# Column means of an 8192 x 8192 matrix: loads in pairs of row groups, the last four groups summed on TensorE alone

## The chip, the core and the metric

The kernel runs on one core of a Trainium2 chip. The time is device time in microseconds. The engines named below are TensorE (PE, its weight loads PEld), VectorE (DVE), ScalarE (ACT), GpSimd (POOL) and SyncE (SP), which here issues the loads and most of the stores. Data move between the chip's main memory and the on-chip memory through 16 DMA engines.

## The reference

```python
def setup_inputs():
    return {"x": np.random.randn(8192, 8192).astype(np.float32)}

def reference(x):
    return np.mean(x, axis=0)
```

The input has 268.4 MB and is read once. The output has 32 KB.

## The kernel before

The 8192 rows are 64 groups of 128 rows (one row of a group per partition, 4 MB a group). A block is 512 columns (`F`), so a group has 16 blocks; `W` is a quarter of a block. `bufs` (L51) holds six rows of 8192 floats per partition: four are landing places, `both` (L52) takes the sum of two of them, `acc` (L53) is the running sum.

Loads all go through `load` (L75) on SP's queue. A load names as its wait the add that reads its buffer last, and each even load from the ninth on also the two loads eight and seven places before it. SP works in order, so a load that waits holds all that are written behind it.

- L111 to L113: the first loads are the last two blocks of group 60 into the tile `early` (512 KB), groups 0 to 3 in one load of 16 MB, groups 4 and 5 in one of 8 MB, and blocks 9 to 13 of group 63 into `early` (1280 KB).
- L114 to L116: VectorE adds groups 0 and 1 to 2 and 3 in an add of 16,384 columns, then 4 and 5 onto these in another (the result lies in `both` and `acc`), and `both` onto `acc`.
- L120 to L133: groups 6 to 55 come in pairs, 8 MB a load, two neighbouring rows of the matrix (64 KB in one stretch) per partition. For each pair VectorE adds the two rows into `both` and `both` into `acc`. After the pairs 24 and 32, GpSimd adds the early pieces of group 63 into `acc` (L129).
- L135 to L138: groups 56 to 59 come one by one; one add each.
- L139 to L144: group 60 is loaded without its last two blocks and added in blocks 0 to 13; of group 61 blocks 7 to 15 are added.
- L146 to L152: group 62 is loaded whole; GpSimd adds its blocks 14, 15 and 8 into `acc` (L148). Group 63 then comes in pieces: blocks 4 to 7, 0 to 3, 14 and 15, and 8.

The function `add` (L94) lets a no-op of ScalarE or GpSimd (L99) wait for the load and for the add ahead, and the add waits for that no-op alone.

TensorE sums over the 128 partitions: a matmul with a 128 x 32 matrix of 1/8192 (`ones`) puts the column sums of up to 512 columns into one of four strips of 32 partitions (L183; each matmul appears as two instructions). Which block goes when is the list `sums`, written by `blocks` (one block per strip) and `spread` (several blocks cut into four equal parts). Its order (L167 to L181) begins with blocks 2 to 4 and 0 to 1 of `acc` and blocks 0 to 6 of group 61, and ends with the pieces of group 63. Four tiles of accumulators fill up: `banks` (blocks 0 to 3, 4 to 7), `wide` (blocks 9 to 13), `two` (14, 15) and `last` (8).

ScalarE copies the accumulators out (L209 to L213; the copies lie inside `both`), VectorE the last one (L214), and five stores write the result, two from ScalarE's queue and three from SP's (L210, L216 to L219). At the end SP waits for loads and stores (`landed`, L220 to L224), and VectorE for one store (L225).

Of the kernel before, what the change touches and what calls it, by code (L numbers as in the profile page):

```python
# [9 lines left out]
def kernel(  # L10
# [2 lines left out]
    x: bass.AP,  # L13
    out: bass.AP,
):

    nc = tc.nc
    f32 = mybir.dt.float32
    M, N = x.shape  # L40
    P = nc.NUM_PARTITIONS
    F = 512
    W = F // 4
    G = M // P
    U = 6
    sync = mybir.DependencyInfo(mybir.DependencyClass.Sync, mybir.DependencyReason.DATA)

    sb = ctx.enter_context(tc.tile_pool(name="sb", bufs=1))
    psp = ctx.enter_context(tc.tile_pool(name="psum", bufs=1, space=bass.MemoryType.PSUM))

    bufs = sb.tile([P, U, N], f32, name="bufs")  # L51
    both = bufs[:, U - 2, :]  # L52
    acc = bufs[:, U - 1, :]  # L53
    ones = sb.tile([P, 32], f32, name="ones")
    early = sb.tile([P, 7 * F], f32, name="early")
    tail = sb.tile([P, W], f32, name="tail")
    warm = sb.tile([P, 32], f32, name="warm")
    nc.gpsimd.memset(ones[:], 1.0 / M)  # L58
    ready = sb.tile([P, 1], f32, name="ready")
    tc.keep_in_program_order(  # L60
        nc.gpsimd.tensor_add(out=ready[:], in0=ones[:, 0:1], in1=ones[:, 1:2]))  # L61
    banks = [psp.tile([P, F], f32, name=f"bank{b}") for b in range(2)]
    wide = psp.tile([P, 2 * F], f32, name="wide")
    two = psp.tile([P, 2 * W], f32, name="two")
    last = psp.tile([P, W], f32, name="last")

    loads = []

    def landed(*inss):

        nop = tc.keep_in_program_order(nc.sync.nop()).ins
        for o in inss:
            tc.add_manual_dep(nop, o.name, sync, reason="SyncE waits")

    def load(dst, src):  # L75
        ins = tc.keep_in_program_order(nc.sync.dma_start(out=dst, in_=src)).ins  # L76
        k = len(loads)
        over = loads[k - 8:k - 6] if k >= 8 and k % 2 == 0 else []
        tc.declare_no_dep(ins, group="loads", keep=over, reason="the reader of the buffer waited")
        for o in over:  # L80
            tc.add_manual_dep(ins, o.name, sync, reason="covers the next load too")
        tc.add_to_no_dep_group("loads", ins)
        loads.append(ins)
        return ins

    def rows(g, n=1):
        return x[g * P:(g + n) * P, :]

    def load_rows(g, u, n):
        return load(bufs[:, u:u + n, :], rows(g, n).rearrange("(p j) c -> p j c", j=n))  # L90

    adds, joins = [], {}

    def add(dst, a, b, dmas):  # L94

        ins = nc.vector.tensor_add(out=dst, in0=a, in1=b).ins  # L96
        if dmas and adds:
            waiter = nc.scalar if len(adds) % 8 > 1 else nc.gpsimd
            nop = joins[waiter] = tc.keep_in_program_order(waiter.nop()).ins  # L99
            for o in dmas + adds[-1:]:  # L100
                tc.add_manual_dep(nop, o.name, sync, reason="the no-op waits")
            for group in ("loads", "adds"):
                tc.declare_no_dep(ins, group=group, reason="the no-op waited")
            tc.add_manual_dep(ins, nop.name, sync, reason="waits for both at once")
        elif adds:
            tc.declare_no_dep(ins, group="loads", reason="the add ahead waited")
        tc.declare_no_dep(ins, group="early", reason="the no-op waited, or the add behind it")
        tc.add_to_no_dep_group("adds", ins)
        adds.append(ins)

    load(early[:, 5 * F:], rows(G - 4)[:, 14 * F:])  # L111
    first, second = load_rows(0, 0, 4), load_rows(4, 4, 2)
    load(early[:, :5 * F], rows(G - 1)[:, 9 * F:14 * F])  # L113
    add(bufs[:, 2:4, :], bufs[:, 2:4, :], bufs[:, 0:2, :], [first])  # L114
    add(bufs[:, 4:6, :], bufs[:, 4:6, :], bufs[:, 2:4, :], [second])
    add(acc, acc, both, [])  # L116
    tc.keep_in_program_order(nc.scalar.copy(out=warm[:], in_=ones[:]))  # L117
    ahead = []
    g = 6
    while g < G - 8:  # L120
        u = (g + 2) % 4
        dma = load_rows(g, u, 2)
        add(both, bufs[:, u, :], bufs[:, u + 1, :], [dma])
        add(acc, acc, both, ahead)
        ahead = []
        if g in (24, 32):
            lo, hi = (0, 4) if g == 24 else (4, 7)
            cols = slice((9 + lo) * F, (9 + hi) * F)
            ins = tc.keep_in_program_order(nc.gpsimd.tensor_add(  # L129
                out=acc[:, cols], in0=acc[:, cols], in1=early[:, lo * F:hi * F])).ins  # L130
            tc.add_to_no_dep_group("early", ins)
            ahead = [ins]
        g += 2  # L133

    while g < G - 4:  # L135
        row = bufs[:, (g + 2) % 4, :]
        add(acc, acc, row, [load(row, rows(g))])
        g += 1  # L138
    for lo, hi, loaded in [(0, 14, 14), (7, 16, 16)]:  # L139
        row = bufs[:, (g + 2) % 4, :]  # L140
        dma = load(row[:, :loaded * F], rows(g)[:, :loaded * F])
        cols = slice(lo * F, hi * F)
        add(acc[:, cols], acc[:, cols], row[:, cols], [dma])
        g += 1  # L144
    r61, r62, r63 = [bufs[:, (g + 1 + j) % 4, :] for j in range(3)]
    load(r62, rows(g))  # L146
    for cols in [slice(14 * F, 16 * F), slice(8 * F, 9 * F)]:
        joined = tc.keep_in_program_order(nc.gpsimd.tensor_add(  # L148
            out=acc[:, cols], in0=acc[:, cols], in1=r62[:, cols])).ins
    g += 1  # L150
    for lo, hi in [(4, 8), (0, 4), (14, 16), (8, 9)]:
        load(r63[:, lo * F:hi * F], rows(g)[:, lo * F:hi * F])  # L152

    sums = []

    def blocks(row, lo, hi):
        for i in range(lo, hi):
            sums.append((banks[i // 4], i % 4, 0, row[:, i * F:(i + 1) * F]))

    def spread(dst, row, lo, hi, part=slice(None)):  # L160
        n = (hi - lo) * W
        for c in range(0, n, F)[part]:
            for q in range(4):
                at = lo * F + q * n + c
                sums.append((dst, q, c, row[:, at:at + min(F, n - c)]))

    blocks(acc, 2, 5)  # L167
    blocks(acc, 0, 2)
    blocks(r61, 0, 7)
    blocks(acc, 5, 8)  # L170
    blocks(r62, 0, 8)
    spread(wide, acc, 9, 14, slice(1))
    blocks(r63, 4, 8)
    spread(wide, r62, 9, 14, slice(1))
    for row in (acc, r62):
        spread(wide, row, 9, 14, slice(1, 2))
    spread(two, acc, 14, 16)
    blocks(r63, 0, 4)
    spread(last, acc, 8, 9)
    spread(two, r63, 14, 16)  # L180
    spread(last, r63, 8, 9)  # L181
    for n, (dst, q, c, cols) in enumerate(sums):
        summed = tc.keep_in_program_order(nc.tensor.matmul(  # L183
            out=dst[32 * q:32 * q + 32, c:c + cols.shape[1]],
# [5 lines left out]
            skip_group_check=True,  # L190
        )).ins

    res = both[:, :2 * F].rearrange("p (b c) -> p b c", b=2)
    res5 = both[:, 2 * F:2 * F + 5 * W]
    res2 = both[:, 4 * F:4 * F + 2 * W]

    def copy(dst, src):
        return tc.keep_in_program_order(nc.scalar.copy(out=dst, in_=src)).ins  # L198

    def store(engine, dst, src, *then):  # L200
        ins = tc.keep_in_program_order(engine.dma_start(out=dst, in_=src)).ins
        for o in then:
            tc.add_manual_dep(ins, o.name, sync, reason="follows that load")
        return ins

    def part(lo, hi):
        return out[lo * F:hi * F].rearrange("(q c) -> q c", q=4)

    copy(res[:, 1, :], banks[1][:])  # L209
    s1 = store(nc.scalar, part(4, 8), res[0:P:32, 1, :], loads[-4])  # L210
    copy(res5, wide[:, :5 * W])
    copy(res[:, 0, :], banks[0][:])
    copied = copy(res2, two[:])  # L213
    ended = nc.vector.tensor_copy(out=tail[:], in_=last[:]).ins  # L214
    landed(*joins.values())
    s5 = store(nc.sync, part(9, 14), res5[0:P:32, :], *loads[-7:-3])  # L216
    s0 = store(nc.sync, part(0, 4), res[0:P:32, 0, :])
    s2 = store(nc.scalar, part(14, 16), res2[0:P:32, :])
    store(nc.sync, part(8, 9), tail[0:P:32, :])  # L219
    landed(loads[-2], joined)  # L220
    landed(loads[-1], copied)
    landed(s0, s5)
    landed(s1, summed)
    landed(s2, ended)  # L224
    hold = tc.keep_in_program_order(nc.vector.nop()).ins  # L225
    tc.add_manual_dep(hold, s0.name, sync, reason="VectorE ends late")

# [29 lines left out]
```

## Time and profile before

| | us |
|---|---|
| median of 3 runs | 628.55 (627.99 to 628.99) |
| profiled execution, first to last instruction (span) | 626.4 |
| median run less the span | 2.15 |
| VectorE busy, 60 instructions | 529.3 |
| TensorE busy, 126 matmul instructions | 13.3 |
| GpSimd busy | 12.0 |
| ScalarE busy | 3.7 |
| read from main memory | 268.44 MB, 429 GB/s over the span |

The profiled execution has no time of its own beside its span; what lies around the span is taken from the median of the runs. In the profile, times count from the start of the span. A line of the chain has a start, a duration, and the engine, tile and line that ran then, or "DMA" for the time from a load's issue to its landing. A line of the timeline has a start, a duration, engine, line, operation, tiles, the number of instructions merged, and in brackets how long the engine had been idle and what ended that. L96 is VectorE's add, L76 a load, L99 the no-op, L183 a matmul, L201 a store.

### The profile page before, as it was taken

How to read it: one execution, taken by the hardware profiler on the slowest of the kernel's cores; microseconds unless marked ns; L12 is line 12 of the kernel's file. 1: busy time of each engine (PE TensorE's matmuls, PEld its weight loads, DVE VectorE, ACT ScalarE, POOL GpSimd, SP SyncE). 2: the span in 40 equal slices, each digit the busy share in tenths (PEclk: the TensorE clock that was granted, in tenths of full speed). 3: DMA queues.
4: the chain of work that ended last, by engine and by line, in shares of the span. 5: the costliest groups of instructions: out<-in, count | busy, mean ns of one | idle time of the engine just before them, and what ended most of it. 6: DMA issues, size and time to landing. Idle time of an engine off the chain costs nothing.

```text
span 626.4 us, 484 instructions
## 1 busy us (share of the span) xinstructions
PE 13.3 (2%) x126; PEld 4.0 (1%) x126; DVE 529.3 (85%) x60; ACT 3.7 (1%) x6; POOL 12.0 (2%) x10
## 2 busy tenths in 40 slices
PE   0000000000000000000000000000000000000008
PEld 0000000000000000000000000000000000000002
DVE  0028999998888998889998899888898888999992
ACT  0000000000000000000000000000000000000001
POOL 0000000000000000020000200000000000000002
PEclk9999999999999999999999999999999999999999
DMA  8999999999999999999999999999999999999997
GB/s 372 465 402 428 459 410 460 402 469 402 469 402 469 402 469 402 469 402 469 402 465 406 439 431 427 444 410 460 402 469 402 469 402 469 402 435 435 419 435 305
DMA packets 5930, 268.50 MB, mean 429 GB/s; under 512 B 660, under 2 KB 668, under 8 KB 1064
## 3 DMA queue, kind: packets, MB, share of 16 engines
q1 hardware_dynamic: 5912, 268.46, 99.3%
q8 instruction: 1, 0.02, 0.0%
q10 hardware_dynamic: 16, 0.01, 0.0%
q14 instruction: 1, 0.01, 0.0%
HBM read 268.44 MB, written 0.03 MB: 429 GB/s over the span
## 4 chain that ended last, share of the span: by engine, by line
DMA 59%; DVE 30%; another core or an unknown queue 10%; issue 0%; SPq 0%; ACTq 0%; PE 0%; POOL 0%; POOLq 0%
DMA bufs<-in_x_dram 59%; DVE bufs L96 30%; SPq L76 0%; ACTq L99 0%; PE last L183 0%; DVE tail L214 0%; POOL ready L61 0%; POOL ones L58 0%; POOLq L99 0%; POOLq L241 0%
## 5 line engine op out<-in xcount | busy, mean ns | idle before, releaser
L96 DVE TENSOR_TENSOR bufs<-bufs 128x8192 f32<-128x8192 f32 (+3 forms) x59 | 529.0, 8966 | 85.9 <-DMA bufs<-in_x_dram 43.0
L183 PE MATMUL bank<-bufs,ones 128*32 128x512 f32 x62 | 10.0, 716 | 610.3 <-DVE bufs L96 610.0
L129 POOL TENSOR_TENSOR bufs<-bufs,early 128x2048 f32<-128x2048 f32 (+1 forms) x2 | 7.9, 3954 | 348.5 <-DVE bufs L96 348.5
L148 POOL TENSOR_TENSOR bufs<-bufs 128x1024 f32<-128x1024 f32 (+1 forms) x2 | 3.6, 1824 | 258.9 <-DMA bufs<-in_x_dram 258.9
L214 DVE COPY tail<-last 128x128 f32<-128x128 f32 x1 | 0.3, 291 | 8.8 <-PE last L183 8.8
L183 PEld LDWEIGHTS bank<-bufs,ones 128*32 128x32 f32 x62 | 2.2, 121 | 616.4 <-issue 614.5
L198 ACT COPY bufs<-bank 128x512 f32<-128x512 f32 x2 | 1.2, 586 | 617.9 <-PE bank L183 617.9
L183 PE MATMUL wide<-bufs,ones 128*32 128x512 f32 (+1 forms) x32 | 2.5, 432 | 0.0
L117 ACT ACT_TABLE_LOAD x1 | 1.3, 1283 | 0.7 <-PEq L241 0.7
L183 PE MATMUL two<-bufs,ones 128*32 128x256 f32 x16 | 1.2, 380 | 0.0
L183 PEld LDWEIGHTS wide<-bufs,ones 128*32 128x32 f32 x32 | 1.0, 110 | 1.8 <-issue 1.8
L183 PE MATMUL last<-bufs,ones 128*32 128x128 f32 x16 | 0.8, 279 | 0.1
L198 ACT COPY bufs<-wide 128x640 f32<-128x640 f32 x1 | 0.7, 692 | 1.1 <-PE wide L183 1.1
L183 PEld LDWEIGHTS last<-bufs,ones 128*32 128x32 f32 x16 | 0.4, 109 | 1.2 <-issue 0.6
L183 PEld LDWEIGHTS two<-bufs,ones 128*32 128x32 f32 x16 | 0.4, 109 | 0.1
L198 ACT COPY bufs<-two 128x256 f32<-128x256 f32 x1 | 0.4, 372 | 0.1
L117 ACT COPY warm<-ones 128x32 f32<-128x32 f32 x1 | 0.2, 217 | 0.0
L61 POOL TENSOR_TENSOR ready<-ones 128x1 f32<-128x1 f32 x1 | 0.2, 193 | 0.1
L58 POOL MEMSET ones<- 128x32 f32 x1 | 0.1, 125 | 0.3 <-POOLq L241 0.3
L241 POOL MEMSET const-float32-0.0<- 128x1 f32 x1 | 0.1, 98 | 0.2 <-issue 0.2
L241 POOL MEMSET const-bfloat16-1.0<- 128x1 bf16 x1 | 0.1, 102 | 0.0
L241 POOL MEMSET const-uint8-127<- 128x1 uint8 x1 | 0.1, 102 | 0.0
(1 smaller groups left out, 0.1 us busy)
## 6 DMA issues: line engine op xcount, KB each, us to landing
bufs<-in_x_dram SPq DMA_DIRECT2D x6, 4096.0 KB, 20.4
bufs<-in_x_dram SPq DMA_DIRECT2D x1, 3584.0 KB
bufs<-in_x_dram SPq DMA_DIRECT2D x2, 1024.0 KB, 18.7
early<-in_x_dram SPq DMA_DIRECT2D x1, 1280.0 KB
early<-in_x_dram SPq DMA_DIRECT2D x1, 512.0 KB
bufs<-in_x_dram SPq DMA_DIRECT2D x1, 512.0 KB, 19.4
bufs<-in_x_dram SPq DMA_DIRECT2D x27, 29.9
bufs<-in_x_dram SPq DMA_DIRECT2D x1, 256.0 KB, 19.7
```

The source lines that it names most:

```text
L58: nc.gpsimd.memset(ones[:], 1.0 / M)
L61: nc.gpsimd.tensor_add(out=ready[:], in0=ones[:, 0:1], in1=ones[:, 1:2]))
L96: ins = nc.vector.tensor_add(out=dst, in0=a, in1=b).ins
L117: tc.keep_in_program_order(nc.scalar.copy(out=warm[:], in_=ones[:]))
L129: ins = tc.keep_in_program_order(nc.gpsimd.tensor_add(out=acc[:, cols], in0=acc[:, cols], in1=early[:, lo * F:hi * F])).ins
L148: joined = tc.keep_in_program_order(nc.gpsimd.tensor_add(out=acc[:, cols], in0=acc[:, cols], in1=r62[:, cols])).ins
L183: summed = tc.keep_in_program_order(nc.tensor.matmul(out=dst[32 * q:32 * q + 32, c:c + cols.shape[1]], lhsT=ones[:], rhs=cols, start=all(( ...
L198: return tc.keep_in_program_order(nc.scalar.copy(out=dst, in_=src)).ins
L214: ended = nc.vector.tensor_copy(out=tail[:], in_=last[:]).ins
L241: nc = _bacc.Bacc("TRN2", target_bir_lowering=False, num_devices=1)
```

## The change

There are no early loads and no tile `early`. All groups up to 61 are loaded in pairs, the first pair too; the places of the pairs alternate (buffers 0 and 1, 2 and 3). Each of the pairs up to 58 is added by VectorE as before in the middle of the kernel, the first straight into `acc`; so VectorE sums groups 0 to 59. Pair 60 is loaded and not added. Group 62 is loaded whole, group 63 in pieces of blocks 0 to 7, 8 to 12, 13 and 14, and 15. GpSimd adds nothing.

TensorE takes all 16 blocks of group 60, of 61, of `acc`, of 62 and of 63, in this order. The accumulators hold blocks 0 to 3, 4 to 7, 8 to 12, 13 and 14, and 15. The copies go to tiles of their own; VectorE copies the second accumulator and the last, ScalarE the other three, all after the whole list of matmuls is written. Four stores go by SP, that of blocks 13 and 14 by ScalarE, and the stores no longer name loads to follow.

```diff
-    load(early[:, 5 * F:], rows(G - 4)[:, 14 * F:])
-    first, second = load_rows(0, 0, 4), load_rows(4, 4, 2)
-    load(early[:, :5 * F], rows(G - 1)[:, 9 * F:14 * F])
-    add(bufs[:, 2:4, :], bufs[:, 2:4, :], bufs[:, 0:2, :], [first])
-    add(bufs[:, 4:6, :], bufs[:, 4:6, :], bufs[:, 2:4, :], [second])
-    add(acc, acc, both, [])
+    def pair(g):
+        u = g % 4
+        dma = load(bufs[:, u:u + 2, :], rows(g, 2).rearrange("(p j) c -> p j c", j=2))
+        return bufs[:, u, :], bufs[:, u + 1, :], dma
+
+    a, b, dma = pair(0)
+    add(acc, a, b, [dma])
...
+    for g in range(2, G - 4, 2):
+        a, b, dma = pair(g)
+        add(both, a, b, [dma])
+        add(acc, acc, both, [])
+    r60, r61, _ = pair(G - 4)
+    r62, r63 = bufs[:, 2, :], bufs[:, 3, :]
+    load(r62, rows(G - 2))
+    for lo, hi in [(0, 8), (8, 13), (13, 15), (15, 16)]:
+        load(r63[:, lo * F:hi * F], rows(G - 1)[:, lo * F:hi * F])
...
+    def spread(dst, row, lo, n):
+        for c in range(0, n * W, F):
             for q in range(4):
-                at = lo * F + q * n + c
-                sums.append((dst, q, c, row[:, at:at + min(F, n - c)]))
+                at = lo * F + q * n * W + c
+                sums.append((dst, q, c, row[:, at:at + min(F, n * W - c)]))
...
+    for row in (r60, r61, acc, r62, r63):
+        blocks(banks[0], row, 0)
+        blocks(banks[1], row, 4)
+        spread(banks[2], row, 8, 5)
+        spread(banks[3], row, 13, 2)
+        spread(last, row, 15, 1)
...
+    copy(0)
+    nc.vector.tensor_copy(out=res[1][:], in_=banks[1][:])
+    copy(2)
+    copied = copy(3)
     ended = nc.vector.tensor_copy(out=tail[:], in_=last[:]).ins
     landed(*joins.values())
...
+    s0 = store(nc.sync, 0, 4, res[0])
+    s4 = store(nc.sync, 4, 8, res[1])
+    s8 = store(nc.sync, 8, 13, res[2])
+    s13 = store(nc.scalar, 13, 15, res[3])
+    store(nc.sync, 15, 16, tail)
+    landed(loads[-2])
     landed(loads[-1], copied)
-    landed(s0, s5)
-    landed(s1, summed)
-    landed(s2, ended)
+    landed(s0, s4)
+    landed(s8, summed)
+    landed(s13, ended)
```

More of the change, by code (lines that the diff above doesn't have):

```diff
@@ L54 @@
     ones = sb.tile([P, 32], f32, name="ones")
-    early = sb.tile([P, 7 * F], f32, name="early")
     tail = sb.tile([P, W], f32, name="tail")
+    res = [sb.tile([P, w], f32, name=f"res{i}") for i, w in enumerate((F, F, 5 * W, 2 * W))]
     warm = sb.tile([P, 32], f32, name="warm")
@@ L61 @@
         nc.gpsimd.tensor_add(out=ready[:], in0=ones[:, 0:1], in1=ones[:, 1:2]))
-    banks = [psp.tile([P, F], f32, name=f"bank{b}") for b in range(2)]
-    wide = psp.tile([P, 2 * F], f32, name="wide")
-    two = psp.tile([P, 2 * W], f32, name="two")
+    banks = [psp.tile([P, w], f32, name=f"bank{b}") for b, w in enumerate((F, F, 2 * F, 2 * W))]
     last = psp.tile([P, W], f32, name="last")
@@ L87, in rows @@
         return x[g * P:(g + n) * P, :]
-    def load_rows(g, u, n):
-        return load(bufs[:, u:u + n, :], rows(g, n).rearrange("(p j) c -> p j c", j=n))
     adds, joins = [], {}
@@ L106, in add @@
             tc.declare_no_dep(ins, group="loads", reason="the add ahead waited")
-        tc.declare_no_dep(ins, group="early", reason="the no-op waited, or the add behind it")
         tc.add_to_no_dep_group("adds", ins)
         adds.append(ins)
-    load(early[:, 5 * F:], rows(G - 4)[:, 14 * F:])
-    first, second = load_rows(0, 0, 4), load_rows(4, 4, 2)
-    load(early[:, :5 * F], rows(G - 1)[:, 9 * F:14 * F])
-    add(bufs[:, 2:4, :], bufs[:, 2:4, :], bufs[:, 0:2, :], [first])
-    add(bufs[:, 4:6, :], bufs[:, 4:6, :], bufs[:, 2:4, :], [second])
@@ L116 @@
-    add(acc, acc, both, [])
-    tc.keep_in_program_order(nc.scalar.copy(out=warm[:], in_=ones[:]))
[L118 to L149, printed above, removed]
@@ L150 @@
-    g += 1
-    for lo, hi in [(4, 8), (0, 4), (14, 16), (8, 9)]:
-        load(r63[:, lo * F:hi * F], rows(g)[:, lo * F:hi * F])
-    sums = []
[L156 to L162, printed above, removed]
-            for q in range(4):
-                at = lo * F + q * n + c
-                sums.append((dst, q, c, row[:, at:at + min(F, n - c)]))
@@ L167 @@
[L167 to L181, printed above, removed]
+    def pair(g):
+        u = g % 4
+        dma = load(bufs[:, u:u + 2, :], rows(g, 2).rearrange("(p j) c -> p j c", j=2))
+        return bufs[:, u, :], bufs[:, u + 1, :], dma
@@ new lines, with blocks @@
+    a, b, dma = pair(0)
+    add(acc, a, b, [dma])
+    tc.keep_in_program_order(nc.scalar.copy(out=warm[:], in_=ones[:]))
+    for g in range(2, G - 4, 2):
[7 more added lines that the diff above has]
+        load(r63[:, lo * F:hi * F], rows(G - 1)[:, lo * F:hi * F])
+    sums = []
+    def blocks(dst, row, lo):
+        for q in range(4):
+            sums.append((dst, q, 0, row[:, (lo + q) * F:(lo + q + 1) * F]))
@@ L191, with copy, store @@
         )).ins
[L193 to L213, printed above, removed]
+    def copy(i):
+        return tc.keep_in_program_order(nc.scalar.copy(out=res[i][:], in_=banks[i][:, :res[i].shape[1]])).ins
+    def store(engine, lo, hi, src):
+        dst = out[lo * F:hi * F].rearrange("(q c) -> q c", q=4)
+        return tc.keep_in_program_order(engine.dma_start(out=dst, in_=src[0:P:32, :])).ins
+    copy(0)
+    nc.vector.tensor_copy(out=res[1][:], in_=banks[1][:])
+    copy(2)
+    copied = copy(3)
     ended = nc.vector.tensor_copy(out=tail[:], in_=last[:]).ins
     landed(*joins.values())
[L216 to L220, printed above, removed]
+    s0 = store(nc.sync, 0, 4, res[0])
[4 more added lines that the diff above has]
+    landed(loads[-2])
     landed(loads[-1], copied)
-    landed(s0, s5)
-    landed(s1, summed)
-    landed(s2, ended)
+    landed(s0, s4)
+    landed(s8, summed)
+    landed(s13, ended)
     hold = tc.keep_in_program_order(nc.vector.nop()).ins
```

## The prediction

> **What bounds the kernel now.** I read the page's busy line, its DMA queues and its chain first, then the chain in order of time, then the timeline of the last 14 us, then the groups by shape. The page:
>
> ```profile
> PE 13.3 (2%) x126; PEld 4.0 (1%) x126; DVE 529.3 (85%) x60; ACT 3.7 (1%) x6; POOL 12.0 (2%) x10
> q1 hardware_dynamic: 5912, 268.46, 99.3%
> ```
>
> The load queue q1 moves packets for 99.3% of 626.4 us, that is 622.0 us; the other 4.4 us are the start before the first packet and the stores' end. No load ever waits long enough for the queue to run dry. VectorE is at 85% and has no share in the rate. The chain in order of time:
>
> ```profile
> 472.10 8.70 DVE bufs L96
> 480.80 0.02 issue
> 480.82 29.93 DMA bufs<-in_x_dram
> 510.75 0.03 ACTq L99
> 510.79 0.02 issue
> 510.81 8.70 DVE bufs L96
> 519.51 0.02 issue
> 519.53 29.92 DMA bufs<-in_x_dram
> 549.44 0.04 ACTq L99
> ...
> 603.45 19.74 DMA bufs<-in_x_dram
> 623.19 0.04 issue
> 623.23 0.47 PE last L183 x8
> 623.70 0.02 issue
> 623.73 0.29 DVE tail L214
> ```
>
> Each 8 MB load is issued when the add that frees its two rows ends, and lands 29.9 us later, because the load ahead of it is still moving. Landings 510.75 and 549.44 are four groups apart: 38.69 us, or 9.673 us per group. The pieces of "DVE" in this chain are therefore no bound: they end 10.6 us before the queue would be empty (29.93 less the 19.35 that a pair moves). What ends the run is the last piece's landing at 623.19, then eight matmuls, one copy, one store. The timeline of TensorE near the end:
>
> ```profile
> 616.28 1.92 PE L183 MATMUL bank<-bufs,ones 128*32 128x512 f32 x16 [0.28 <-DMA bufs<-in_x_dram]
> 618.02 1.04 PE L183 MATMUL wide<-bufs,ones 128*32 128x512 f32 x8
> 618.88 1.04 PE L183 MATMUL bank<-bufs,ones 128*32 128x512 f32 x8
> 619.74 1.48 PE L183 MATMUL wide<-bufs,ones 128*32 128x512 f32 x24
> 621.03 0.61 PE L183 MATMUL two<-bufs,ones 128*32 128x256 f32 x8
> 621.46 1.04 PE L183 MATMUL bank<-bufs,ones 128*32 128x512 f32 x8
> 623.73 0.29 DVE L214 COPY tail<-last 128x128 f32<-128x128 f32 x1 [8.83 <-PE last L183]
> 624.04 0.50 SPq L201 DMA_DIRECT2D out_dram<-tail  x1
> ```
>
> Starts give TensorE's pace: eight instructions of 512 columns 0.86 us (618.02 to 618.88), eight of 256 columns 0.43 (621.03 to 621.46), sixteen of 128 columns 0.43 (1.29 less 0.86). The sums start at 609.98, and there the weight loads show four instructions per 0.86 us (half pace) until 613.41, four per 0.43 after it. 616.28 is also the landing of group 62.
>
> **The change part by part.** All sums are made against the profiled execution, span 626.4; the median run is 628.55, so 2.15 us lie outside the span, and I keep them.
>
> *The load stream.* The bytes stay the same, so only packet sizes and gaps count. The trace's packet records give the time of one packet: 64 KB 2.420 us, 32 KB 1.218, 10 KB 0.385 median and 0.420 mean (all 128 in the early piece), 8 KB 0.313, 4 KB 0.159 median and 0.193 mean, 2 KB 0.084; each load has eight per DMA engine. The check: group 63's eleven blocks in pieces of 4, 4, 2 and 1 give 8 x (0.313 + 0.313 + 0.159 + 0.084) = 6.95, and the landings 616.28 and 623.23 are 6.95 apart.
> - Early pieces removed: 8 x 0.193 + 8 x 0.420 = 4.90 us leave the stream ahead of group 56. In before, 549.44 is the landing of groups 0 to 55 and the early pieces, so after it is 544.54. The slow mean of the 4 KB piece may belong to being first and not to its size; then 8 x (0.193 - 0.159) = 0.27 stays with the first pair. With a rest for the unlike start I take 0 to 0.33 us back.
> - Groups 56 to 61 become three pairs: 6 x 9.673 = 58.04, landing of pair 60 at 602.58. Single groups cost (616.28 - 549.44) / 6.875 = 9.722 each, so pairs save 0.05 apiece.
> - Group 62 stays single: 9.72, at 612.30.
> - Group 63 now brings all 16 blocks as 8, 5, 2, 1. A 16 KB packet isn't in the loads; a line through 10 KB and 28 KB (0.385 and 1.067) gives 0.613. 8 x (0.613 + 0.385 + 0.159 + 0.084) = 9.93, or 10.21 with the early piece's 0.420. Last landing 622.23.
> - With both upper ends, 622.84. Before it was 623.23. So the stream ends 0.39 to 1.00 us earlier; I take 0.70, the middle, since neither excess has a second row.
>
> *Queues.* There are 36 loads for 40; the load of a pair waits for the add that reads its rows, as before. At the start only pairs 0 and 2 are queued (39 us of work); pair 0 lands near 21.9, VectorE adds it in 8.7, and the third pair is issued near 31, some 10 us before the queue ends. At the end group 62 and all pieces of 63 wait for the first add of pair 58 (landing 583.2, add 8.7: 591.9), while pair 60 is still moving until 602.6. That is the cover; without it each microsecond of lateness would be one of time. The five issues take about 0.35 us each and hold nobody.
>
> *VectorE.* 59 adds of 8192 columns at 8.70, two per pair, 17.4 of each 19.35. POOL's two adds of early pieces (4.49 and 3.42) leave, and with them the longer adds beside them; both were under the stream. acc is complete at 583.2 + 17.5 = 600.7, and TensorE wants it at 611.4. POOL's two adds of group 62 leave as well.
>
> *TensorE.* 240 matmul instructions for 126. One row is 3 x 0.86 (eight blocks and the wide part of five) + 0.22 + 0.43 + 0.22 = 3.44 us. It starts at pair 60's landing, cold: 16 instructions at half pace cost 1.72 more. Rows 60, 61, acc, 62 and the first eight blocks of 63 take 1.72 + 4 x 3.44 + 1.72 = 17.2 us. The stream brings blocks 8 to 12 of group 63 at 9.72 + 4.90 + 3.08 = 17.7 us after pair 60. So TensorE arrives 0.5 us ahead and the last landing rules again: then 0.47 for the last eight, as before. To the end TensorE needs 17.2 + 1.08 + 0.43 + 0.47 = 19.2 us, the stream 19.65 + 0.47 = 20.1. The cover is 0.9 us; this is the thin place of the change.
>
> The trace shows one warm-up, 3.43 us at half pace (609.98 to 613.41), while the page's clock row says 1.00 throughout. [...]
>
> *Copies and stores.* ScalarE copies bank 0 (0.59) early, VectorE bank 1: no row, between the 0.29 of 128 columns and the 0.69 of ScalarE's 640; I take 0.69. Both are over before 621.5. The copy of the wide bank (0.69) ends near 622.3, its store on SP (0.63, from "622.43, two in 1.26") near 622.9; the tail's store wants SP at 623.34. So it isn't held up, with 0.4 us to spare; if it is, 0.1 to 0.5 us are paid. The VectorE hold now waits for a store that is long over: 0, at most 0.1 either way.
>
> Sum: last landing -0.70, the rest as before: tail's store issued at 623.34 for 624.04, span 625.7, with 2.15 outside it 627.85. I write 627.9.
>
> **The rivals.**
> [...]
> - *TensorE far behind (slower).* It decides from 2.9 us of extra TensorE work, that is 0.9 of cover and 2.0 from 627.85 to 629.81: a half pace of 9.2 us or more, or eight wide instructions in 1.0 us instead of 0.86. [...] Half pace to the end would give 34.4 for 20.1: 642. For it: rows of four groups in one uninterrupted run, which this trace never shows while five loads move. Against it: at 616.28 to 622.3 the pace held while loads moved.
> - *The stream is slower at the pairs' rate.* 0.03 us more per group over 62 groups would add 1.9 to 627.85: 629.8. For it: single slices of the page swing from 402 to 469 GB/s. Against it: 38.69 and 38.70 repeat from 123.7 to 549.4, two and two pairs.
> - *The early pieces cost more than their packets* (a turn of the queue at start or at 62 us): another 0.6 off, 627.2, faster. For it: the first 10 us move 367 GB/s. Against it: the start has no reason to end with them.
> - *No effect at all*, the upper ends taken and the tail's store held up: 628.3, inside the forecast's own width.
>
> **How the numbers follow.** About 0.2%, 1.26 us, is what a measurement can tell from no change here: faster is under 627.29, slower over 629.81. Chances: forecast 0.57 (its own range 627.2 to 628.7), one window more 0.14, TensorE far behind 0.13, slower stream 0.08, early pieces dearer 0.08. Faster: the last and 0.04 of the forecast's low side, 0.12. Slower: 0.13 and 0.08, and 0.01 of the one-window case, 0.22. Same: 0.66. The range reaches from 627.1 (1.00 off and 0.45 for runs that differ by 0.5 from their median) to 630.2, which takes in the slower stream and part of TensorE far behind, and leaves out less than 2 in 10.
>
> **What would show it.** Right: landing of pair 60 at 602.6 to 603.0, group 62 at 612.3 to 612.8, the last piece at 622.2 to 622.9; q1 again over 99%; TensorE's first matmul right at pair 60's landing, with waits on DMA in group 63; VectorE's last add near 600.7. [...]

## The result, and the profile after

The changed kernel takes 629.64 us (median of 16 runs, 629.14 to 630.35), the kernel before 628.50 in the same runs: ratio 1.002, interval 1.0013 to 1.0026. It is slower by 1.1 us, where 0.7 us of gain was forecast. The median span went from 626.4 to 627.65; what lies outside the span stayed at 1.9 to 2.0. So the loss is inside the span. The page of the changed kernel (span 627.8):

```profile
PE 20.5 (3%) x240; PEld 8.0 (1%) x240; DVE 513.8 (82%) x61; ACT 3.1 (0%) x5; POOL 0.5 (0%) x6
q1 hardware_dynamic: 5216, 268.47, 99.1%
q8 instruction: 2, 0.03, 0.0%
q14 instruction: 1, 0.01, 0.0%
```

The loads are again over 99% of the span. The two lines below them are instruction fetches: packets of 16 KB on q8 and of 8 KB on q14, which by the order of the packets (sorted into 16 rows further down) go through the same 16 DMA engines as the loads. Before had one of each on its page too, and their place in time is what counts. The trace's packet records put before's at 622.6 us (q8, around the last landing) and 626.0 (q14, after all stores), and after's at 462.5 (q14), 615.6 and 623.5 (q8). The chain of the changed kernel, in order of time:

```profile
457.45 30.69 DMA bufs<-in_x_dram
488.14 0.03 ACTq L70
...
496.92 29.92 DMA bufs<-in_x_dram
...
535.62 29.94 DMA bufs<-in_x_dram
...
574.33 29.92 DMA bufs<-in_x_dram
604.25 0.14 issue
604.39 6.09 PE bank L118 x40
610.47 0.22 PE last L118 x8
610.69 3.22 PE bank L118 x40
```

One load, that issued at 457.45, took 30.69 us for the 29.92 of the loads behind it: 0.77 late, with the 8 KB packet at 462.5 in it, and nothing behind it won the time back. Pair 60 landed at 604.25; 602.58 to 602.9 was forecast. Group 63's pieces, behind the 16 KB packet at 615.6, in the timeline (start, duration, line, operation, and in brackets what the engine waited for):

```profile
622.57 0.16 PEld L118 LDWEIGHTS bank<-bufs,ones 128*32 128x32 f32 x8 [0.74 <-DMA bufs<-in_x_dram]
623.81 0.16 PEld L118 LDWEIGHTS bank<-bufs,ones 128*32 128x32 f32 x8 [0.22 <-DMA bufs<-in_x_dram]
624.44 0.16 PEld L118 LDWEIGHTS last<-bufs,ones 128*32 128x32 f32 x8 [0.48 <-DMA bufs<-in_x_dram]
625.25 0.51 SPq L133 DMA_DIRECT2D out_dram<-tail  x1
```

TensorE waits for all three last pieces, so the loads still set the end. The last one came at 624.44, before's at 623.23: 1.21 of the profiled 1.4 us. The other 0.2 us lie behind the issue of the tail's store, which is at 625.25 for 624.04 and so 1.21 late too. TensorE was not far from setting the end itself: it began the sums of group 63 at 620.83 and had 3.22 us of work before the last eight, so it could have started these at 624.05 at the earliest.

### The profile page after: what moved, and what is told of

It reads as the page before. It is cut to its first block, busy times and chain, and to the rows that moved or that the text cites. A ratio compares the mean times of both kernels' runs of the same rounds, so it can differ in the third digit from the quotient of the medians.

```text
span 627.8 us, 690 instructions
## 1 busy us (share of the span) xinstructions
PE 20.5 (3%) x240; PEld 8.0 (1%) x240; DVE 513.8 (82%) x61; ACT 3.1 (0%) x5; POOL 0.5 (0%) x6
## 3 DMA queue, kind: packets, MB, share of 16 engines
q1 hardware_dynamic: 5216, 268.47, 99.1%
## 4 chain that ended last, share of the span: by engine, by line
DMA 75%; DVE 21%; PE 3%; issue 0%; ACTq 0%
DMA bufs<-in_x_dram 75%; DVE bufs L67 21%; PE bank L118 3%; PE last L118 0%; ACTq L70 0%; DVE tail L139 0%
## 5 line engine op out<-in xcount | busy, mean ns | idle before, releaser
L67 DVE TENSOR_TENSOR bufs<-bufs 128x8192 f32<-128x8192 f32 x59 | 512.8, 8692 | 89.5 <-ACTq L70 41.8
L118 PE MATMUL bank<-bufs,ones 128*32 128x512 f32 (+2 forms) x200 | 20.0, 546 | 604.4 <-DMA bufs<-in_x_dram 604.4
L118 PEld LDWEIGHTS bank<-bufs,ones 128*32 128x32 f32 x200 | 6.9, 120 | 615.5 <-issue 614.5
L129 ACT COPY res<-bank 128x512 f32<-128x512 f32 (+2 forms) x3 | 1.6, 550 | 621.1 <-PE bank L118 621.1
L118 PE MATMUL last<-bufs,ones 128*32 128x128 f32 x40 | 2.1, 275 | 0.0
## 6 DMA issues: line engine op xcount, KB each, us to landing
bufs<-in_x_dram SPq DMA_DIRECT2D x31, 29.9
```

Of the source, the lines that this page charges most:

```text
L118: summed = tc.keep_in_program_order(nc.tensor.matmul(out=dst[32 * q:32 * q + 32, c:c + cols.shape[1]], lhsT=ones[:], rhs=cols, start=all(( ...
L129: return tc.keep_in_program_order(nc.scalar.copy(out=res[i][:], in_=banks[i][:, :res[i].shape[1]])).ins
```

## The experiments

Four theories were put against each other. A: TensorE's 16 KB fetch holds one DMA engine's share of the loads, and a load lands with its slowest engine. B: the loads in pairs, at the start above all, are slower by themselves. C: TensorE's longer list is the loss. D, after the first four runs: the 8 KB fetch belongs to VectorE's program and costs in the same way. The table has what the runs gave; "last" is where the last eight matmuls start in the profiled execution, 0.04 or 0.05 us behind the last piece's landing in every kernel but e2; the fetches are from the packet records (us from the start of the span, those before 630).

| kernel | time, us (before beside it) | median span | TensorE (weight loads with it), VectorE instructions | 8 KB at | 16 KB at | last |
|---|---|---|---|---|---|---|
| before | 628.5 | 626.4 | 252, 60 | 626.0, 628.1 | 622.6 | 623.23 |
| after | 629.64 (628.50) | 627.65 | 480, 61 | 462.5 | 615.6, 623.5 | 624.44 |
| e1_before_extra_fetch | 629.60 (628.33) | 627.7 | 508, 60 | 627.6, 629.6 | 343.4, 622.6 | 624.64 |
| e2_after_head_of_before | 632.01 (628.33) | 630.2 | 480, 59 | 628.7 | 617.8, 625.2 | 626.52 |
| e3_after_two_rows_summed | 629.72 (628.33) | 627.0 | 192, 61 | 462.4 | 629.0 | 623.81 |
| e4_before_head_in_pairs | 628.94 (628.33) | 627.1 | 252, 62 | 466.5, 628.4 | 622.2 | 623.87 |
| f1_after_copy_on_scalar | 630.60 (628.39) | 628.7 | 480, 60 | 626.2 | 614.3, 623.6 | 624.42 |
| f2_before_one_more_vector | 629.18 (628.39) | 627.2 | 252, 61 | 485.7, 628.9 | 622.2 | 623.74 |
| f3_after_no_fetch | 629.98 (628.39) | 627.5 | 192, 60 | 624.8 | 629.4 | 623.02 |
| g1_after_scalar_copy_hold | 629.39 (628.34) | 627.4 | 480, 60 | 627.3 | 614.6, 623.4 | 624.05 |
| g2_after_loads_63_sums | 630.25 (628.34) | two groups | 252, 60 | 626.0 | 622.2 | 622.84 |
| g3_before_no_hold | 629.39 (628.34) | 627.4 | 252, 60 | 625.6, 629.4 | 622.6 | 623.30 |
| h1_after_loads_60_sums | 630.16 (628.29) | two groups | 240, 60 | 626.0 | 622.0 | 622.92 |
| h2_after_loads_63_again | 628.60 (628.29), one execution | 626.7 | 252, 60 | 626.4 | 622.4 | 623.27 |
| h3_after_loads_early_pe | 630.44 (628.10) | 628.5 | 252, 60 | 626.1 | 622.0 | 624.27 |
| h4_after_loads_no_fetch_hold | 629.15 (628.31) | 626.3 | 192, 60 | 626.0 | 628.6 | 622.95 |

**One fetch more on the kernel before.** 64 small products after the add of pair 30:

```diff
+        if g == 30:
+            for i in range(64):
+                extra = tc.keep_in_program_order(nc.tensor.matmul(
+                    out=spare[0:32, 0:32], lhsT=ones[:], rhs=ones[:], start=True, stop=True, ...))
+                if i == 0:
+                    tc.add_manual_dep(extra, adds[-1].name, sync, ...)
```

> The kernel before, with 64 small matmuls (256 TensorE instructions, a 32 x 32 product each, result unused) that run after the add of pair 30. Theory A (instruction fetches share the DMA engines with the loads: one 16 KB fetch packet, 1.07 us in the changed kernel's trace, holds one engine's load queue for about 0.5 us, and a load lands with its slowest engine): one fetch packet of 16 KB appears near 310 us, the next landings come 0.4 to 1.0 us late and stay late, time 0.4 to 1.0 us over the kernel before. Theory B (the loss is in the start and the first loads): within 0.2 us of the kernel before. Theory C (TensorE's tail is the loss): within 0.2 us.

It came 1.27 us over the kernel before (ratio 1.0020, 1.0011 to 1.0028). The chain, in order of time, has the price at one place:

```profile
289.90 27.43 DMA bufs<-in_x_dram
326.11 31.34 DMA bufs<-in_x_dram
366.23 29.93 DMA bufs<-in_x_dram
```

The load with the 16 KB packet at 343.4 lands 1.4 us late (31.34 for 29.93), and the loads behind it keep the delay. A holds, dearer than its range by a little, with the packet at 343.4 and not near 310; B and C, which gave nothing here, don't explain this run.

**The head of before on the changed kernel.** Groups 0 to 5 in loads of 16 and 8 MB:

```diff
+    first, second = load_rows(0, 0, 4), load_rows(4, 4, 2)
+    add(bufs[:, 2:4, :], bufs[:, 2:4, :], bufs[:, 0:2, :], [first])
+    add(bufs[:, 4:6, :], bufs[:, 4:6, :], bufs[:, 2:4, :], [second])
+    add(acc, acc, both, [])
...
-    for g in range(2, G - 4, 2):
+    for g in range(6, G - 4, 2):
```

> The changed kernel with the first six groups loaded as before, 16 MB and 8 MB, and added in two wide adds; no early pieces, tail as changed. Theory A (instruction fetches): at most 0.4 us faster than the changed kernel, so 0.7 to 1.2 us over the kernel before. Theory B (start and first loads, which moved 0.8 us between the forecast landing of ten groups, 99.58, and the measured 100.38): 0.6 to 0.9 us faster than the changed kernel, 0.2 to 0.5 us over the kernel before. Theory C (TensorE's tail): no change, 1.1 over.

All three theories missed: the median is 3.7 us over the kernel before, and the profiled execution, the slowest of the five, has a span of 631.4 for 626.4. Three things add up in it. The first is the loads: without the early pieces the queue has only 8 MB behind the 16 MB load, and the next load waits for a wide add of 17.2 us. In the table of stretches the columns are span, length, busy time of the engines, granted clock, DMA share and GB/s; first this kernel, then the kernel before:

```profile
59.00:64.00 5.00, 0.00 (x0) 0.00 (x0) 2.85 (x2) 0.00 (x0) 0.00 (x0) 1.00 0.85 301
```

```profile
59.00:64.00 5.00, 0.00 (x0) 0.00 (x0) 2.81 (x2) 0.00 (x0) 0.00 (x0) 1.00 0.97 390
```

The DMA engines are busy 0.85 of these 5 us for 0.97, and 64 KB packets take up to 3.65 us there for 2.42; they stay a little slower up to 130 us, and why was not followed. In all the last piece lands at 626.11, 2.9 us after before's. The second is TensorE: from pair 60's landing on it never waits, and it starts its last eight matmuls at 626.52, 0.4 us after that landing. From its first row's start to the second's are 6.31 us, to the third's 3.44 more. So in this run C holds: an excess of 2.87 us is half of the time at half pace, which by this estimate lasted 5.7 us for the 3.43 that the prediction took. The third is the end: VectorE's 8 KB packet is at 628.7, among the last stores, and from the last eight matmuls to the end of the span are 4.85 us for 3.34 in the changed kernel. The run says nothing on B, but it tells what the early 1280 KB did in before: they kept the queue full there.

**Most of TensorE's list left out.**

```diff
-    for row in (r60, r61, acc, r62, r63):
+    for row in (r62, r63):
```

> The changed kernel with the sums of rows 60, 61 and acc left out on TensorE (the loads and adds all stay; the output holds groups 62 and 63 alone), so that TensorE has 192 instructions for 480 and starts at group 62's landing. Theory A: no 16 KB fetch before the last landing, the pieces of group 63 land 0.4 to 0.6 us earlier than in the changed kernel after group 62, time 0.4 to 0.6 us under the changed kernel. Theory B: no change, 1.1 us over the kernel before. Theory C: the time falls to the kernel before's or under it, with the landings where they were.

The span fell by 0.65 us, from 627.65 to 627.0, with no 16 KB packet ahead of the end, as A said; the time did not fall, because the part outside the span grew from 1.9 to 2.6 us. There the fetch had only moved behind the kernel's end (629.0). That was not foreseen; that the fetch is what lengthens this part is likely, but no run tests it alone.

**Pairs at the head of before.** Groups 0 to 5 in three pairs, early pieces and tail kept.

```diff
-    first, second = load_rows(0, 0, 4), load_rows(4, 4, 2)
+    first, second = load_rows(0, 2, 2), load_rows(2, 0, 2)
...
-    add(bufs[:, 2:4, :], bufs[:, 2:4, :], bufs[:, 0:2, :], [first])
-    add(bufs[:, 4:6, :], bufs[:, 4:6, :], bufs[:, 2:4, :], [second])
+    add(acc, bufs[:, 2, :], bufs[:, 3, :], [first])
+    add(both, bufs[:, 0, :], bufs[:, 1, :], [second])
...
-    g = 6
+    g = 4
```

> The kernel before with groups 0 to 5 loaded as three pairs, the early pieces and the tail as before. Theory A: within 0.3 us of the kernel before. Theory B: 0.5 to 0.8 us over the kernel before, with landings of the first ten groups late by as much. Theory C: no change.

0.6 us over the kernel before, which B had asked for; but the landings told otherwise: the delay is in one load of 30.90 us with an 8 KB packet at 466.5, not in the first ten groups. Here VectorE has 62 instructions. That made theory D.

**VectorE's count, one edit each way.** In the changed kernel ScalarE copies the second accumulator; in the kernel before VectorE gets one copy more.

```diff
-    nc.vector.tensor_copy(out=res[1][:], in_=banks[1][:])
+    copy(1)
```

```diff
+    spare = sb.tile([P, 32], f32, name="spare")
+    tc.keep_in_program_order(nc.vector.tensor_copy(out=spare[:], in_=ones[:]))
     ended = nc.vector.tensor_copy(out=tail[:], in_=last[:]).ins
```

> The changed kernel with the copy of the second accumulator on ScalarE, so that VectorE has 60 instructions for 61 in the page's busy line. Theory D (an instruction fetch of 8 KB at 462 us belongs to VectorE: it came in each kernel with 61 or 62 VectorE instructions and in none with 59 or 60): no such packet before the last landing, pair 60 lands 0.7 to 1.0 us earlier than in the changed kernel (604.25 there). The end is still set by the DMA engine that TensorE's 16 KB fetch at 616 us holds, so the span falls by 0 to 0.4 us only. Theory E (the 8 KB packet has nothing to do with VectorE's program): packet and landing stay, span unchanged.

> The kernel before with one more VectorE instruction, a copy of 128 x 32 numbers nobody reads, put behind the last add: 61 for 60. Theory D: an 8 KB fetch packet appears in the middle of the stream (460 to 490 us), the landings behind it come 0.7 to 1.0 us late, time and span 0.6 to 1.0 us over the kernel before. Theory E: within 0.2 us of the kernel before, no packet.

One copy of 128 x 32 numbers, put behind the last add, made the kernel before 0.8 us slower (ratio 1.0013, 1.0004 to 1.0022), and the delay is in the middle of the stream, long before that copy runs:

```profile
441.89 29.92 DMA bufs<-in_x_dram
480.59 30.73 DMA bufs<-in_x_dram
520.10 29.93 DMA bufs<-in_x_dram
```

The 8 KB packet is at 485.7. In the changed kernel with 60 VectorE instructions it left the stream, as D said, and the last piece landed where it had (the last eight matmuls start at 624.42). But the span rose by 1 us instead of falling: the packet now came at 626.2, among the last stores. What SP waited for, first this kernel, then the changed one:

```profile
SPq L46 <- DMA out_dram<-res: 1.7, 2, 1.1
```

```profile
SPq L46 <- DMA out_dram<-res: 0.7, 2, 0.6
```

**Where VectorE's fetch goes at the end.** In the first run, on top of the copy by ScalarE, VectorE's last wait (the "hold" of before's L225) is set on a later store; the second takes it out of the kernel before.

```diff
-    tc.add_manual_dep(hold, s0.name, sync, reason="VectorE ends late")
+    tc.add_manual_dep(hold, s8.name, sync, reason="VectorE ends late")
```

```diff
-    hold = tc.keep_in_program_order(nc.vector.nop()).ins
-    tc.add_manual_dep(hold, s0.name, sync, reason="VectorE ends late")
```

> The changed kernel with the second accumulator copied by ScalarE (60 VectorE instructions) and VectorE's last wait set on the store of blocks 8 to 12 instead of the store of blocks 0 to 3, which ends before the last landing. Fetch theory: with 60 instructions VectorE fetches its 8 KB about 1.2 us after its last branch; in the run with the copy alone (span 628.7) that met the last stores. Now it comes after 627 us, the stores land as in the changed kernel, span 627.2 to 627.7, time 629.1 to 629.6. Rival (ScalarE's third copy delays the stores by itself): span stays at 628.4 or above.

> The kernel before without VectorE's last wait. Fetch theory: VectorE's 8 KB fetch starts near 625.2 us instead of 626.3, meets the last stores, span 0.4 to 1.1 us longer than the kernel before's 626.4. Rival (the wait is of no use): within 0.2 us.

Both came as the fetch theory had it: 627.4 for 628.7, and 627.4 for 626.4. In the kernel before without the wait, SP's waits have a line that the kernel before hasn't:

```profile
SPq L250 <- DMA out_dram<-tail: 1.3, 1, 1.3
```

The fetch at 625.6 holds up the tail's store; with the wait it is at 626.0, behind it.

**Both fetches out, and the rest of the loss.** The changed kernel with rows 62 and 63 alone on TensorE, 60 VectorE instructions, and VectorE's last wait on the first store (f3) or on that of blocks 8 to 12 (h4).

> The changed kernel with both fetches taken out of the stream: copy of the second accumulator on ScalarE, and the sums of rows 60, 61 and acc left out on TensorE (the output holds groups 62 and 63 alone). Fetch theory (A with D): span 0.6 to 1.0 us under the one with two rows summed (627.0 median), so 626.0 to 626.4, at or under the kernel before's 626.4; the time outside the span stays near 2.8 us as there. Theory B (the start in pairs costs by itself): span stays at 626.8 or above.

> The changed loads with no fetch before the last store lands: 48 sums (192 TensorE instructions, rows 62 and 63; rows 60, 61 and acc are left out of the output), second accumulator copied by ScalarE (60 VectorE instructions), VectorE's last wait on the store of blocks 8 to 12. Fetch theory: last piece at 622.6 to 623.1, spans in one group at 626.0 to 626.5, against 627.5 for the one with the wait on the first store and 626.4 for the kernel before; TensorE's fetch comes behind the span, so that the time is 2.4 to 2.9 us over the span, 628.5 to 629.3. Rival (the loads make a second group of spans by themselves): spans of 627.5 and more again.

With the wait on the first store the last piece was in time (623.02), but VectorE's fetch at 624.8 met the stores: 627.5, a miss by its numbers. With the later wait all eleven executions had spans from 626.1 to 626.5. The chain of that run at its end:

```profile
621.06 1.92 PE bank L118 x24
622.99 0.44 PE last L118 x8
```

So the changed loads, with no fetch ahead of the last store, give 626.3, no worse than before's 626.4. B has no room left as a loss against before. The run doesn't speak on C, since three of TensorE's five rows are left out. An estimate for the whole list: pair 60's last packet ends at 602.85 in h4 and 603.79 in the changed kernel, where TensorE could have started its last eight matmuls 20.26 us later (624.05); that gives 623.1 for h4's 622.95, so that TensorE and not the loads would set the end, at about 626.5. As in e3, TensorE's own fetch then lies behind the span and the time outside is 2.85, so this is no faster kernel: 629.15.

**With as many TensorE instructions as before.** Three runs meant to have both the forecast span and the usual 1.9 us outside: 15 or 12 sums of acc, then rows 62 and 63; or 15 products on the small matrix in the first microseconds and then these rows. As in h4, ScalarE copies the second accumulator and VectorE's last wait is on the store of blocks 8 to 12.

```diff
+    sums = sums[48:48 + 15] + sums[72:]
```

> The one above with as many TensorE instructions as the kernel before has (63 sums, 252 instructions: 15 sums of acc, all of rows 62 and 63; rows 60, 61 and the rest of acc are left out of the output). Fetch theory: no fetch packet before 622 us, the last piece lands at 622.6 to 623.2, span 625.9 to 626.5, time 627.8 to 628.5 with 1.9 to 2.0 us outside the span: what the forecast gave for the changed kernel. Rival (the loads in pairs are slower by themselves): span 627 or above.

> As the run with 63 sums, but 60 sums (240 TensorE instructions; 12 sums of acc, all of rows 62 and 63, the rest is left out). The run with 63 had spans from 626.2 to 626.6 and from 627.8 to 629.2. If TensorE's own fetch made the two (it starts at 622.4 us, about 230 instructions in, between the last two pieces' landings, so that a small shift puts it ahead of the last piece or of the stores), then with 12 instructions fewer it starts only with the last piece's sums, behind the last landing: last piece at 622.6 to 623.0 in every run and never late, while the stores may meet the fetch; spans in one group, 626.0 to 628. If the two groups come from the loads, both stay as they were.

> The kernel with 63 sums once more, for a profile of its slower executions. If the fetch is the cause: in an execution with a span of 627.8 or more, the landings up to pair 60 are as in the one of 626.2 (612.9 for group 62), and what is late comes after 622 us, behind the 16 KB packet. If the loads are the cause: group 62 lands 1 us late or more.

> As the run with 63 sums, but the 15 extra TensorE products run in the first 10 us on the matrix of 1/8192 instead of on acc at 601 us, so that TensorE has 252 instructions and no work between 10 us and group 62's landing (rows 60, 61 and acc are left out of the output). If the second group of spans came from TensorE's clock (in the 63-sums run it worked from 601 to 606 us, idled 6.8 us and was granted 0.50 again from 610 on, so that a second warm-up of changing length begins at 613): one group of spans, 626.0 to 626.6, time 627.9 to 628.5, at the kernel before's. If the loads or the fetch make the second group: spans of 627.8 and more appear again.

The first gave spans of 626.2 to 626.6 in four executions and of 627.8 to 629.2 in eight, the second the same two groups, against its expectation that 12 instructions would part them; the repeat, one execution of 626.7 and 628.60 us, met the early group again. The third had only the late group, 628.1 to 628.9, against its expectation. Its timeline shows that group from inside:

```profile
613.30 5.08 PE L124 MATMUL bank<-bufs,ones 128*32 128x512 f32 x40 [610.58 <-DMA bufs<-in_x_dram]
618.41 1.90 PE L124 MATMUL bank<-bufs,ones 128*32 128x512 f32 x16
621.17 1.93 PE L124 MATMUL bank<-bufs,ones 128*32 128x512 f32 x24 [0.86 <-DMA bufs<-in_x_dram]
624.27 0.43 PE L124 MATMUL last<-bufs,ones 128*32 128x128 f32 x8 [1.17 <-DMA bufs<-in_x_dram]
```

Group 62 and the piece of blocks 8 to 12 are in time (613.30 and 621.17, h4: 613.16 and 621.06); the last piece comes 1.3 us late, behind the 16 KB packet at 622.0. TensorE's fetch came 8.7 us after its first sum of group 62, and 8.9 to 9.2 us after it in the profiles of the other three. The tail's store, late by that, then met VectorE's fetch at 626.1 as well (SP waits 1.5 us for it). That the late executions of g2 and h1 are of the same kind is likely but not seen: no profile fell on one.

**A slip of the experiment.** To have the pairs at before's head with 60 VectorE instructions, the first two pairs were added in one wide add.

```diff
+    add(bufs[:, 4:6, :], bufs[:, 2:4, :], bufs[:, 0:2, :], [second, first])
+    add(acc, acc, both, [])
```

> The kernel before with groups 0 to 5 in three pairs (627.15 span, 62 VectorE instructions), with the first two pairs added in one wide add and the last copy on ScalarE, so that VectorE has 60 instructions. Theory D: no 8 KB packet in the stream, span 626.2 to 626.6, time within 0.25 us of the kernel before. Theory B: still 0.6 us over the kernel before.

645.64 us: the add waits for both pairs and frees all four buffers only at its end, so that the queue moved 118 GB/s from 42 to 62 us. It can't speak on D: VectorE had a wait instruction of its own besides the 60, and the packet came at 483.1. What B asked is answered by e4 and f2, where 62 and 61 instructions bring the same packet and the spans are 627.1 and 627.2, with and without pairs at the head.

## Why the prediction was wrong

- **The step that failed: "The bytes stay the same, so only packet sizes and gaps count."** The stream also carries instruction fetches, and a fetch adds its time to one engine's queue (0.78 us behind the 8 KB one in the changed kernel, next point). TensorE's 240 matmul instructions for 126 were counted as TensorE's time alone, and VectorE's one copy more (61 for 60) at nothing. The 240 moved a 16 KB fetch from 622.6, where the loads were nearly over, to 615.6; the copy put an 8 KB fetch at 462.5. On the kernel before the prices are 1.3 us (e1) and 0.8 us (f2).
- **The two don't add up in the changed kernel, because they fall on two DMA engines.** The last eight matmuls start at 624.44 with both, at 623.81 with the 8 KB alone (e3), at 624.05 and 624.42 with the 16 KB alone (g1, and f1, which lost 0.45 us more in slow packets from 158 to 236 us) and at 622.95 with none (h4). That is 0.9, 1.1 to 1.5, and 1.5 for both. The packet records don't name the engine, but an engine's packets follow each other within 0.02 us, so that they can be sorted into 16 rows. Behind the 8 KB packet one row is 0.78 us behind the slowest of the others (at the start of group 62, 613.50 for 612.73); the 16 KB packet at 615.59 lies in another row. The last load packet ends at 623.39 in the first, at 623.97 in the second and by 622.63 in the other fourteen, and the last piece's landing, at 624.40, follows the latest. Taking only VectorE's copy away, with the fetch behind the stores, gains 0.25 us (g1, 627.4).
- **The stream's sum was right, at its upper end or a little above.** The range was 622.23 to 622.84, and 622.53 was taken; without a fetch the last sums start at 622.84 (g2) and 622.95 (h4), 0.04 behind the landing. Pair 60 came later than its 602.58 to 602.9: its last packet ends at 602.67 (g2) to 602.85 (h4), and 0.46 later, as in the changed kernel, is 603.1 to 603.3. The first pair landed at 22.51 in the changed kernel, where the low end (602.58 less 30 pairs of 19.346) has 22.2 and 0.33 more gives 22.5: most of the slow first packets' time belongs to being first. So 0.3 to 0.4 of the 0.7 us gain is there, against some 1.5 us that the fetches take.
- **Queues and VectorE: right.** Loads stay at 29.9 but for the one with the fetch and two early ones (30.19 and 30.15, landings 61.44 and 100.37), during each of which all 16 engines had a slow round of packets (2.5 to 2.6 us for 2.42) with no fetch near; g1 and h1 have no such rounds, and their cause is open. The pieces wait for nobody, and the sums of acc were never waited for.
- **TensorE: right in the end by luck, wrong in a size.** In the timeline the rows start at 604.39, 610.50 and 613.94, 6.11 and 3.44 us apart. The excess of 2.67 is half of the time at half pace, which so lasted 5.3 us, to about 609.7, for the 3.43 assumed. TensorE reached group 63 at 620.83, 16.4 us after its start for the 15.5 counted. That used up the 0.9 us of cover; it still waited for each later piece only because the 16 KB fetch made the stream late, and in e2 it set the end. The chance of 0.14 for "one window more" stood for a half pace of twice the 3.43 us of before, which was assumed; no run shows one that comes in steps of 3.43. By the same estimate it lasted 5.7 us in e2 and 4.3 in h4 (rows at 613.16 and 618.73). The granted clock is 1.00 through the stretches of before (610.0 to 613.4) and of the changed kernel (604.4 to 610.3), so what makes the half pace there is not shown.
- **"The VectorE hold ... 0, at most 0.1 either way": right in number, wrong in reason.** With 61 instructions VectorE has fetched at 462 us, and the page shows no later fetch of it that the wait could move (not tested). With 60 the same wait is worth 1.0 us (g3) and its place 1.3 us (g1 against f1).
- **The end of the span** grew by 0.2 us that was not in the sum. SP's wait for ScalarE's store of blocks 13 and 14 ends 2.2 us after the last eight matmuls start, for 2.0 with before's store of blocks 14 and 15. That store, ScalarE's first of the run, took 1.08 us to issue, before's second one 0.51; that this is the reason is argued, not shown.

## What to carry to other kernels

In a kernel that the load stream bounds (q1 at 99.1% here), an instruction is also a transfer (one copy more on VectorE brought one of 8 KB, f2): count each engine's instructions, look at the instruction queues in the list of DMA queues, and find when their packets come, before a change is called free. Here one instruction more moved a fetch into the stream (f2: from 626.0 to 485.7, 0.8 us), one fewer moved it among the last stores (f1: from 462.5 to 626.2, the span 1 us longer), and a wait at an engine's end placed it behind them (g1: 627.3, the span 1.3 us shorter than f1's). Leaving work out as a test moved fetches too (e3: TensorE's from 615.6 to 629.0, with 2.6 us outside the span for 1.9), so compare the landings and the part of the time outside the span, not the time alone.

## What was not expected of the hardware

- A fetch of 8 KB delays a load by 0.77 to 0.99 us and one of 16 KB by 1.4 (e1), although the packets themselves last 0.33 and 1.07. The load packet behind the fetch on the same engine is slower too: 64 KB took 3.08 us for 2.42 behind the 8 KB, and 16 KB took 1.11 for 0.61 behind the 16 KB. The 16 KB packets are TensorE's, the 8 KB ones VectorE's. TensorE itself does not show the cost (its weight loads keep their pace of four per 0.43 us across the packet at 615.6); the loads do.
- TensorE's first fetch came after 198 to 259 instructions that the trace shows, where it had more than 192; VectorE's in the stream after 47 in each kernel that has one there. It is there only in the kernels whose traces have 68 or more VectorE instructions, waits and the lines behind the program's end included; the others have 66 or 67. Why the length of the rest decides is open.
- The part of the time outside the span is 2.4 to 2.85 us (medians) for 1.8 to 2.0 in the three kernels where TensorE had 192 instructions and its 16 KB fetch came behind the span (628.6 to 629.4). That one makes the other is likely, not tested.
